# Trainium2 kernel: the end of layer 0 with five gated tiles fetched and split ahead, steps kept back for the seam behind pair 9, and the group norm at the head of the tail

## The chip, the cores and the metric

One core of a Trainium2 chip runs one launch of the kernel. The metric is the device time of a launch in microseconds (us), the median of several runs.

## The reference, cut to what matters

A trunk of two layers. Layer 0 is RWKV-7 time mixing, layer 1 differential attention; both have memory attention, a SiLU gate and an output projection. In layer 0 there are 512 prompt rows and 32 sample rows (544 columns in the kernel), 24 heads of 64 that are worked in 12 pairs, and 4 memory heads:

```
p, qm, gate = split(rmsnorm(x) @ w_in)
ps = p + mu * (p_prev - p); r, k, v, pw, pa = split(ps)
S = S * w + (S @ -kk) (kk * a)^T + v k^T; y = S @ r
y = groupnorm(y) * ln_w + ln_b + sum(r * k * r_k) * v
out = concat(y, softmax(qm @ mk^T) @ mv) * silu(gate)
x = x + out @ w_out
```

The outputs hold p's last row too (the shift state, for prompt and sample).

## The kernel before, in words

**Products.** A float32 product runs as three products of fp32r parts: hi x hi, lo x hi, hi x lo, where hi is the value cast and lo is what is left of it. ACT makes hi (CAST), VectorE (DVE) or GpSimd (POOL) subtracts and makes lo. Weights come as raw blocks of 1024 x 128, and are cast to whi and wlo as put-off work. One step of a product is one matmul of 128 x 128 by 128 x 272, and a block of weights takes 48 steps: 8 row blocks x 2 halves of the columns x 3 parts. The main stream (`stream`) of layer 0 gives such steps (tile `ps_g`, operands `hh`, `hl`, `whi`, `wlo`), and they are laid between everything else.

**The order.** Every instruction is issued in the program's order on its engine, and a helper (`tie`, L103) keeps that order; so nearly all rows carry L103 and are told apart by tiles. Layer 0 is a chain over 12 pairs. A pair has 23 entries (PLAN) of two halves; each half does a piece of the chain (`chain`: state updates, tiles `ps_c`, `avz`, `SB`), a piece of another pair's preparation (`prep`, `at`, `inv`, `mrg`, `val`: tiles `rkv`, `bk`, `bt`, `ps_v`, `ps_at`), of the group norm and the gate of the pair before (`rsq`, `fin`: tiles `yt`, `q`, `sg`, `bv`, `ps_y`), then one piece of put-off work (`some`, from the head of the list `self.later`), and then as many steps of the main stream as the planner's estimate of time gives (L1428 to L1465; MAIN is 0.126 us for a step). `until` empties the list up to a named piece. MPLAN says at which entries of pairs 10 and 11 the steps of the four memory heads (`mem_steps`, tiles `cmt`, `mhk`, `mq`, `ps_ck`, `ps_mm`, `mp`) stand.

**The seam behind pair 9** (`pr + 3 == NPAIR`, L1464). Three pieces of the preparation of pair 11 run with nothing between them, the put-off list is emptied, the memory of the preparation (`ca`) is freed and the memory heads' (`mem0a`) is opened in its place. Two transposes take the shift state (`shc`) into PSUM (`ps_sh`), ACT copies it (`sho`), and SP issues its two output transfers. The memory head's first load is `cmt`.

**The end of layer 0.** `put` stores each gated tile of 128 x 544 (`sg`) to a scratch in DRAM (`oscr`), 16 tiles in all. Behind pair 11 TAIL lists the last pieces: four pieces of `fin` (gates), `rsq` (the group norm's statistics), four times `split`, four pieces of `fin`, `out`, with 6 steps behind each. The steps come from the rest of the main stream and then from the output projection (`w_out`). `w_out` fetches gated tiles four at a time (`fetch`: `lo<-oscr`, 272 KB), and `gated` (L1159 to L1163) casts hi on ACT and makes lo in place, on DVE for an even tile and on POOL for an odd one (L1162). The projection's first two blocks are worked together: tiles 0 to 3 against block 0 (24 steps) and against block 1 (24), then tiles 4 to 7 against both, then the second eight of OUT_ORDER.

Of the kernel before, what the change touches and what calls it, by code (L numbers as in the profile page):

```python
# [17 lines left out]
P = 128  # L18
# [9 lines left out]
MH = 4  # L28
# [45 lines left out]
MPLAN = {10: [(0, 0), (1, 0), (2, 0), (3, 0), (4, 0), (5, 0), (6, 0), (6.5, 1), (7, 0), (8, 0), (9, 0), (10, 0), (10.5, 0), (12.5, 1),  # L74
# [10 lines left out]
TAIL = (("fin", 6), ("fin", 6), ("fin", 6), ("fin", 6), ("rsq", 6), ("split", 6), ("split", 6), ("split", 6), ("fin", 6),  # L85
        ("split", 6), ("fin", 6), ("fin", 6), ("out", 6))
# [19 lines left out]
class Trunk:  # L106
# [768 lines left out]

    def state_out(self, S, dst):
        nc, p = self.nc, self.rk0
        ps = self.psm.tile([P, 4, P], F32, tag="m", name="ps_so")
        self.te.transpose(ps[:, 0, :], S[:], self.ident[:])
        so = p.tile([P, 64], F32, tag="so", name="so", bufs=1)  # L880
        for h in range(2):
            hc = slice(64 * h, 64 * h + 64)
            self.ae.copy(so[hc, :], ps[hc, 0, hc])
        self.se.dma_start(dst.rearrange("h v k -> (h v) k"), so[:])
# [32 lines left out]
    def put(self, g, t):  # L917
        if not self.o1:
            self.se.dma_start(self.oscr[g // 8][:, g % 8, :], t[:])
# [239 lines left out]
    def gated(self, g, hi, lo, t):  # L1159

        self.ae.copy(hi[:], t)
        (self.nc.gpsimd if g % 2 else self.ve).tensor_tensor(lo[:], t, hi[:].bitcast(F32), ALU.subtract)  # L1162
        return hi, lo  # L1163

# [6 lines left out]
    def w_out(self, i, p, order, consume, extra=None, o=None):  # L1171
# [5 lines left out]
        def fetch():  # L1177
            if left:
                g = left.pop(0)
                came.append((g, self.fetch(p, g)))  # L1180

        def ahead(n):
            for _ in range(n):
                if came:
                    g, t = came.pop(0)
                    o[g] = self.gated(g, *t)
                    fetch()

        for _ in range(NGATED):
            fetch()  # L1190
# [65 lines left out]
    def layer0(self, mem):  # L1256
# [6 lines left out]
        with ExitStack() as ctx:  # L1263
# [69 lines left out]
            mems = [{} for _ in range(MH)]  # L1333
# [94 lines left out]
            for pr in range(NPAIR):  # L1428
                mplan = MPLAN.get(pr, ())
                took = [HOP + sum(us for x in y for kind, d, us, _ in x if 0 <= pr + d < NPAIR) for y in PLAN]  # L1430
                load = [HOPV[k % 3] + sum(us for x in y for kind, d, _, us in x if 0 <= pr + d < NPAIR) for k, y in enumerate(PLAN)]
                whole = sum(took) + MEMPE * len(mplan) / 12 + MAIN * each[pr]
# [4 lines left out]
                t, left, spent = 0.0, each[pr], 0.0  # L1437
                for k, y in enumerate(PLAN):
                    go("chain", pr)
                    t += HOP  # L1440
                    spent += HOPV[k % 3]
                    for half, x in enumerate(y):
                        for kind, d, us, vus in x:
                            if 0 <= pr + d < NPAIR and kind != "full":
                                go(kind, pr + d)
                                t += us
                                spent += vus
                        for at, h in mplan:
                            if at == k + half / 2:
                                if h not in mit:  # L1450
                                    mit[h] = self.mem_steps(mems[h], 0, h, self.ma)
                                    next(mit[h])
                                next(mit[h], None)
                                t += MEMPE / 12
                        if FULL not in x:
                            spent += self.some(room * (k + (half + 1) / 2) + 0.4 - spent)
                        while left and t + MAIN / 2 < (due[k + 1] if half else (due[k] + due[k + 1]) / 2):
                            next(main)
                            t += MAIN
                            left -= 1  # L1460
# [3 lines left out]
                if pr + 3 == NPAIR:  # L1464
                    for _ in range(3):  # L1465
                        go("prep", pr + 2)
                    while self.later:
                        self.later.pop(0)[0]()
                    ca.close()
                    self.ma = self.pool("mem0a", 1, ctx=ma, side="right")  # L1470
                    ps = self.psm.tile([P, 512], F32, tag="m", name="ps_sh")
                    so = self.ma.tile([NPROJ, 2, P], F32, name="sho")
                    for q in range(2):
                        self.te.transpose(ps[:NPROJ, q * P : q * P + P], self.shc[:, q, :], self.ident[:])
                    self.ae.copy(so[:], ps[:NPROJ, :256].rearrange("p (q c) -> p q c", q=2))
                    for q, n in ((0, 3), (1, 9)):
                        self.se.dma_start(o[n][0, 0].rearrange("(j p) -> j p", p=P), so[:, q, :])
# [5 lines left out]
            ma.close()  # L1483
            self.mp = self.pool("mem1", 1, ctx=mctx, side="right")
            mh, ml = self.mem_tiles()
            rctx.close()
        self.x1 = self.pool("x1", 1).tile([P, KT, T], F32, name="x1")
        with ExitStack() as ctx:
# [35 lines left out]
            wout, ahead = self.w_out(0, p, OUT_ORDER, consume, residual)  # L1524

            def both():
                yield from main
                for _ in range(2):
                    self.early.append(self.load(*self.ahead.pop(0)))
                yield from wout  # L1530
# [285 lines left out]
    def run(self):  # L1816
# [6 lines left out]
        self.mem = {}  # L1823
# [64 lines left out]
```

## Time and profile before

| | before |
|---|---|
| median of 3 runs | 1451.4 us (1451.32 to 1452.59) |
| the profiled execution, its own time | 1452.73 us |
| its span in the profile | 1451.0 us |
| TensorE's mean granted clock | 0.986 |
| pairs 9, 10 and 11 | about 562.7 to 706 us of the span |

A page of the profile covers one execution. PE is TensorE's matmuls, PEld its weight loads, SPq the engine SP's queue, which issues the DMAs. In a row of a timeline stand the start and the length in us, the engine, the operation, out<-in, the shape and xcount; in brackets how long the engine idled before it and what ended that (`<-`). Rows of the waits name the engine, what it was to do and whom it waited for, with the total, the times and the longest. Rows of stretches give each engine's busy time. The granted clock is the share of full speed that TensorE was given.

### The profile page before, as it was taken

The numbers are of one execution on the slowest core, as the hardware profiler recorded it, in microseconds if no ns is written. First come the engines' busy times: TensorE is split into PE (matmuls) and PEld (weight loads), VectorE is DVE, ScalarE is ACT, GpSimd is POOL, SyncE is SP. The second block draws the span as 40 slices with busy tenths as digits, with TensorE's granted clock in tenths as the row PEclk, the third lists the DMA queues.
The fourth block names the chain that finished last, engine by engine and source line by source line (L and its number), as shares of the span: only waits on it lengthen the run. The fifth ranks groups of instructions, "written<-read, shape, count | busy, mean of one in ns | idle before, by whom it ended". The sixth has DMA issues, their size and how long they took to land.

```text
span 1451.0 us, 31979 instructions
## 1 busy us (share of the span) xinstructions
PE 1397.4 (96%) x11906; PEld 1318.0 (91%) x11906; DVE 919.9 (63%) x2337; ACT 835.6 (58%) x2293; POOL 388.2 (27%) x846
## 2 busy tenths in 40 slices
PE   6998899999999999899999999999999999999997
PEld 5997899999999998788899999999999999999997
DVE  6565667787777887575743566664465745657533
ACT  6664667667776777455543366653565546664322
POOL 2025676566866567500120030000000001000200
PEclk9998999999999999999999999999999999999999
DMA  6442123323223222232554473323323222332321
GB/s 217 124 135 73 27 62 92 81 73 78 63 78 96 69 73 66 77 91 84 174 157 131 132 201 103 84 75 92 113 69 95 80 84 81 89 98 67 97 88 70
DMA packets 266533, 139.20 MB, mean 96 GB/s; under 512 B 57657, under 2 KB 256578, under 8 KB 266378
## 3 DMA queue, kind: packets, MB, share of 16 engines
q1 hardware_dynamic: 266378, 137.16, 33.4%
q8 instruction: 94, 1.54, 0.5%
q14 instruction: 61, 0.50, 0.1%
HBM read 110.98 MB, written 22.78 MB: 92 GB/s over the span
## 4 chain that ended last, share of the span: by engine, by line
PE 80%; DVE 7%; ACT 6%; issue 2%; POOL 2%; DMA 2%; SPq 1%; DVEq 0%; ACTq 0%; POOLq 0%
PE ps_g L103 57%; PE ps_c L103 4%; PE ps_s L103 2%; PE ps_o L103 2%; PE ps_at L103 2%; PE ps_mm L103 1%; PE ps_v L103 1%; DVE wlo L103 1%; PE ps_mo L103 1%; SPq L103 1%; PE ps_aT L103 1%; POOL u L723 1%; PE ps_ss L103 1%; PE ps_yc L103 1%; POOL tm L721 1%
## 5 line engine op out<-in xcount | busy, mean ns | idle before, releaser
L103 PE MATMUL ps_g<-hh,wlo 128*128 128x272 f32 x1808 | 539.5, 298 | 1.4 <-DVE wlo L103 1.4
L103 PE MATMUL ps_g<-hh,whi 128*128 128x272 f32 x1808 | 538.8, 298 | 0.0
L103 PE MATMUL ps_g<-hl,whi 128*128 128x272 f32 x1808 | 533.5, 295 | 0.0
L103 DVE TENSOR_TENSOR wlo<-raw,whi 128x512 fp32r<-128x512 f32 x322 | 224.1, 709 | 199.7 <-ACT whi L103 195.7
L103 PEld LDWEIGHTS ps_g<-hh,wlo 128*128 128x128 f32 x1808 | 342.8, 190 | 5.8 <-DVE wlo L103 2.0
L103 PEld LDWEIGHTS ps_g<-hh,whi 128*128 128x128 f32 x1808 | 343.6, 190 | 4.1
L103 PEld LDWEIGHTS ps_g<-hl,whi 128*128 128x128 f32 x1808 | 343.2, 190 | 3.9 <-issue 0.6
L103 ACT CAST whi<-raw 128x512 fp32r<-128x512 f32 x322 | 195.0, 617 | 180.5 <-PE ps_g L103 103.6
L721 POOL TENSOR_TENSOR tm<-u,m 102x84 f32<-102x84 f32 (+23 forms) x372 | 158.0, 425 | 181.1 <-DMA m<-sc 152.9
L723 POOL TENSOR_TENSOR u<-u,tm 102x84 f32<-102x84 f32 (+23 forms) x372 | 159.4, 429 | 29.1
L103 PE MATMUL ps_g<-lo,whi 128*128 128x272 f32 x512 | 148.6, 290 | 2.1 <-DVE lo L103 1.9
L103 PE MATMUL ps_g<-hi,whi 128*128 128x272 f32 x512 | 149.5, 292 | 0.8 <-ACT hi L103 0.8
L103 PE MATMUL ps_g<-hi,wlo 128*128 128x272 f32 x512 | 148.7, 290 | 0.9 <-DVE wlo L103 0.9
L1162 POOL TENSOR_TENSOR lo<-og,hi 128x544 fp32r<-128x544 f32 x8 | 13.7, 1713 | 485.8 <-DVE og L103 350.6
L103 PEld LDWEIGHTS ps_g<-lo,whi 128*128 128x128 f32 x512 | 97.2, 190 | 2.9 <-DVE lo L103 2.4
L103 PEld LDWEIGHTS ps_g<-hi,whi 128*128 128x128 f32 x512 | 97.2, 190 | 1.0 <-ACT hi L103 1.0
L103 PEld LDWEIGHTS ps_g<-hi,wlo 128*128 128x128 f32 x512 | 97.1, 190 | 1.1 <-DVE wlo L103 1.1
L103 DVE SCALAR_TENSOR_TENSOR SB<-ps_c,dl,sd 64x64 f32<-64x64 f32 x168 | 47.4, 282 | 47.4 <-PE ps_c L103 42.1
L103 ACT COPY sv<-ps_c 64x64 f32<-64x64 f32 x192 | 39.3, 205 | 39.0 <-PE ps_c L103 37.2
L103 ACT ACTIVATE pt<-ps_s,snm 128x128 f32<-128x128 f32 (+3 forms) x96 | 50.7, 529 | 18.1 <-DVE snm L103 17.0
L103 ACT ACTIVATE sg<-ps_g 128x272 f32<-128x272 f32 x64 | 25.3, 395 | 59.8 <-PE ps_g L103 59.5
L103 ACT COPY raw<-ps_g 128x272 f32<-128x272 f32 x74 | 28.6, 386 | 32.5 <-PE ps_g L103 31.8
(366 smaller groups left out, 2600.6 us busy)
## 6 DMA issues: line engine op xcount, KB each, us to landing
raw<-in_rw_in_dram SPq DMA_DIRECT2D x114, 256.0 KB
raw<-in_df_in_dram SPq DMA_DIRECT2D x112, 256.0 KB
raw<-in_w_out_dram SPq DMA_DIRECT2D x64, 256.0 KB
m<-sc SPq DMA_DIRECT2D x36, 128.0 KB
oscr<-sg SPq DMA_DIRECT2D x16, 272.0 KB
lo<-oscr SPq DMA_DIRECT2D x16, 272.0 KB
raw<-in_w_mem_k_dram SPq DMA_DIRECT2D x16, 256.0 KB
raw<-in_w_mem_v_dram SPq DMA_DIRECT2D x16, 256.0 KB
```

The lines of the kernel that those rows point to most:

```text
L103: return lambda *a, **k: self.trunk.tie(self, issue(*a, **k))
L721: nc.gpsimd.tensor_tensor(tm[:, :n, :wd], u3[:, :n, kx : kx + 1].to_broadcast(sh), m3[:, kx : kx + 1, kx + 1 :].to_broadcast(sh), ALU.mult)
L723: nc.gpsimd.tensor_tensor(u3[:, :n, kx + 1 :], u3[:, :n, kx + 1 :], tm[:, :n, :wd], ALU.add)
L1162: (self.nc.gpsimd if g % 2 else self.ve).tensor_tensor(lo[:], t, hi[:].bitcast(F32), ALU.subtract)
```

## The change

- The two transposes of `shc` (37 x 128 each) become one of 74 x 128, with one copy and the two transfers, as `shift_out`, and move from the seam to entry 13 of pair 10 (SHIFTED).
- Of pair 9's 144 main steps 24 (KEPT) aren't planned in it. Eight of them run behind each of the three pieces of `prep` in the seam.
- MPLAN of pair 10: memory head 0's steps from the second on (the one with `ps_ck`) stand an entry later, up to its last.
- In pair 10 five gated tiles (0 to 4) are fetched singly, in entries 1, 3, 5, 7 and 9, into a memory of their own (`wo0e`). Their hi (ACT) and lo (DVE) are put-off work: one in entry 18 of pair 10, four in entries 1, 5, 9 and 13 of pair 11. The projection gets them as made.
- `gated` makes layer 0's lo on DVE always; POOL takes odd ones only in layer 1.
- TAIL: all four `split` go, and 54 steps stand behind the first `fin` after `rsq`. `fetch` only fetches tiles that are stored already.
- `rctx` (layer 0's state) is closed ahead of the opening of `mem1`.

```diff
+SHIFTED, KEPT = 13, 24
+EARLY = 5
+SPLIT = {10: (18,), 11: (1, 5, 9, 13)}
-MPLAN = {10: [(0, 0), (1, 0), (2, 0), (3, 0), (4, 0), (5, 0), (6, 0), (6.5, 1), (7, 0), (8, 0), (9, 0), (10, 0), (10.5, 0), (12.5, 1),
+MPLAN = {10: [(0, 0), (2, 0), (3, 0), (4, 0), (5, 0), (6, 0), (6.5, 1), (7, 0), (8, 0), (9, 0), (10, 0), (11, 0), (11.5, 0), (12.5, 1),
-TAIL = (("fin", 6), ("fin", 6), ("fin", 6), ("fin", 6), ("rsq", 6), ("split", 6), ("split", 6), ("split", 6), ("fin", 6),
-        ("split", 6), ("fin", 6), ("fin", 6), ("out", 6))
+TAIL = (("fin", 6), ("fin", 6), ("fin", 6), ("fin", 6), ("rsq", 6), ("fin", 54), ("fin", 6), ("fin", 6), ("out", 6))
...
+    def shift_out(self):
+        ps = self.psm.tile([P, 512], F32, tag="m", name="ps_sh")
+        so = self.ma.tile([2 * NPROJ, P], F32, name="sho")
+        self.te.transpose(ps[: 2 * NPROJ, :P], self.shc[:].rearrange("p q j -> p (q j)"), self.ident[:])
+        self.ae.copy(so[:], ps[: 2 * NPROJ, :P])
+        for q, n in ((0, 3), (1, 9)):
+            self.se.dma_start(self.o[n][0, 0].rearrange("(j p) -> j p", p=P), so[q * NPROJ : q * NPROJ + NPROJ, :])
...
     def put(self, g, t):
+        self.out.add(g)
...
         self.ae.copy(hi[:], t)
-        (self.nc.gpsimd if g % 2 else self.ve).tensor_tensor(lo[:], t, hi[:].bitcast(F32), ALU.subtract)
+        (self.nc.gpsimd if g % 2 and self.o1 else self.ve).tensor_tensor(lo[:], t, hi[:].bitcast(F32), ALU.subtract)
         return hi, lo
+    def put_split(self, tiles):
+        hi, lo, t = tiles
+        self.put_off(lambda: self.ae.copy(hi[:], t))
+        self.last_split = self.put_off(lambda: self.ve.tensor_tensor(lo[:], t, hi[:].bitcast(F32), ALU.subtract), LATER)
...
-        def fetch():
-            if left:
+        def fetch(n=1):
+            while left and len(came) < n and (self.o1 or left[0] in self.out):
                 g = left.pop(0)
                 came.append((g, self.fetch(p, g)))
...
+                kept = KEPT if pr + 3 == NPAIR else 0
-                whole = sum(took) + MEMPE * len(mplan) / 12 + MAIN * each[pr]
+                whole = sum(took) + MEMPE * len(mplan) / 12 + MAIN * (each[pr] - kept)
-                t, left, spent = 0.0, each[pr], 0.0
+                t, left, spent = 0.0, each[pr] - kept, 0.0
...
+                        if half and pr == NPAIR - 2 and k == SHIFTED:
+                            self.shift_out()
+                        if half and pr == NPAIR - 2 and k % 2 and len(came) < EARLY:
+                            came.append(self.fetch(early, OUT_ORDER[len(came)]))
+                        if half and k in SPLIT.get(pr, ()):
+                            self.put_split(came[len(made)])
+                            made[OUT_ORDER[len(made)]] = came[len(made)][:2]
...
                     for _ in range(3):
                         go("prep", pr + 2)
+                        fill(KEPT // 3)
...
+                    early = self.pool("wo0e", 1, ctx=mctx, side="right")
...
             ma.close()
+            rctx.close()
             self.mp = self.pool("mem1", 1, ctx=mctx, side="right")
             mh, ml = self.mem_tiles()
-            rctx.close()
...
-            wout, ahead = self.w_out(0, p, OUT_ORDER, consume, residual)
+            wout, ahead = self.w_out(0, p, OUT_ORDER, consume, residual, made)
...
+                self.until(self.last_split)
                 yield from wout
```

The order that results, at three places. First PE in the seam: `ps_v<-ident,rkv` and `ps_bt` are the transposes of `prep`, `ps_g` are main steps. Before:

```order
L103 MATMUL ps_c<-sv,bt 128x128
L103 MATMUL ps_yc<-sv,at_90 64x64 x16
L103 MATMUL ps_v<-ident,rkv 128x128 x4
L103 MATMUL ps_bt<-ident,bk 128x128 x4
L103 MATMUL ps_sh<-ident,shc 37x128 x2
L103 MATMUL ps_c<-avz,at_91 128x128
```

The change, from the last of the 16 main steps behind the rkv transposes on:

```order
L105 MATMUL ps_g<-hh,whi 128x272
L105 MATMUL ps_bt<-ident,bk 128x128 x4
L105 MATMUL ps_g<-hl,whi 128x272
L105 MATMUL ps_g<-hh,wlo 128x272
L105 MATMUL ps_g<-hh,whi 128x272
L105 MATMUL ps_g<-hl,whi 128x272
L105 MATMUL ps_g<-hh,wlo 128x272
L105 MATMUL ps_g<-hh,whi 128x272
L105 MATMUL ps_g<-hl,whi 128x272
L105 MATMUL ps_g<-hh,wlo 128x272
L105 MATMUL ps_c<-avz,at_91 128x128
```

The shc transposes are gone from here, and 24 main steps stand between the rkv transposes and the chain's next product. `ps_ck` stood 5 main steps and the chain's pieces behind that product, and now stands 18 main steps behind it.

Second, SP's transfers in the seam (`raw` are weights, `cmt`, `mhk`, `mhv`, `cmv` the first memory head's loads, `lo_9362` and `lo_9411` the first two gated tiles). Before:

```order
L103 DMA oscr_340<-sg_83 128x544
L103 DMA out_dram<-sho 37x128 x2
L103 DMA cmt<-in_cache_mem_k_dram 128x2x128
L103 DMA mhk<-mkv_354 128x256
L103 DMA mhv<-mkv_878 128x256
L103 DMA cmv<-in_cache_mem_v_dram 128x2x128
```

The change:

```order
L105 DMA oscr_340<-sg_83 128x544
L105 DMA cmt<-in_cache_mem_k_dram 128x2x128
L105 DMA mhk<-mkv_354 128x256
L105 DMA mhv<-mkv_878 128x256
L105 DMA cmv<-in_cache_mem_v_dram 128x2x128
L105 DMA raw<-in_rw_in_dram 128x4x128 x2
L105 DMA lo_9362<-oscr_339 128x544
L105 DMA lo_9411<-oscr_339 128x544
```

cmt stands right behind the store of a gated tile; sho's two rows are in pair 10 now.

Third, DVE at the start of the output projection (`nt` and `q` are the group norm's reciprocal root, `yt` the normed values, `bv` the gated ones). Before:

```order
L103 SCALAR_TENSOR_TENSOR q_101<-nt_10638,q_101 128x20
L103 TENSOR_TENSOR lo_10589<-lo_10589,hi_10588 128x544
L103 SCALAR_TENSOR_TENSOR sg_83<-sg_83,ps_g 128x272
L103 TENSOR_TENSOR wlo<-raw,whi 128x512 x2
L103 TENSOR_TENSOR lo_10595<-lo_10595,hi_10594 128x544
L103 TENSOR_TENSOR lo_10656<-lo_10656,hi_10655 128x544
L103 TENSOR_TENSOR yt_102<-yt_102,q_101 128x640
L103 TENSOR_TENSOR lo_10688<-lo_10688,hi_10687 128x544
L103 SCALAR_TENSOR_TENSOR bv_103<-ps_y,PA,bv_103 128x512
```

The change:

```order
L105 SCALAR_TENSOR_TENSOR q_101<-nt_10665,q_101 128x20
L105 TENSOR_TENSOR yt_102<-yt_102,q_101 128x640
L105 SCALAR_TENSOR_TENSOR sg_83<-sg_83,ps_g 128x272
L105 TENSOR_TENSOR wlo<-raw,whi 128x512 x2
L105 TENSOR_TENSOR lo_10616<-lo_10616,hi_10615 128x544
L105 TENSOR_TENSOR lo_10619<-lo_10619,hi_10618 128x544
L105 TENSOR_TENSOR lo_10622<-lo_10622,hi_10621 128x544
L105 TENSOR_TENSOR lo_10625<-lo_10625,hi_10624 128x544
L105 SCALAR_TENSOR_TENSOR bv_103<-ps_y,PA,bv_103 128x512
```

yt comes first, and the four lo between wlo and bv are those of tiles 5 to 8; those of tiles 0 to 4 stand in pairs 10 and 11.

More of the change, by code (lines that the diff above doesn't have):

```diff
@@ L1183, in ahead @@
             for _ in range(n):
+                fetch()
                 if came:
@@ L1186, in ahead @@
                     o[g] = self.gated(g, *t)
-                    fetch()
-        for _ in range(NGATED):
-            fetch()
+                    fetch(depth)
+        depth = 4 if self.o1 else NGATED
+        fetch(depth)
         half = [[g for g in order if g // 8 == q] for q in range(2)]
@@ L1331, in add_mems @@
                     add(None, src, h * P, make)
-            mems = [{} for _ in range(MH)]
+            mems, came, made = [{} for _ in range(MH)], [], {}
             rw_gate = lambda pr, j: add_gate(pr, sts[j], RW_PROJ + 512 + j * P, j % 2)
@@ L1469, in layer0 @@
                     ca.close()
+                    early = self.pool("wo0e", 1, ctx=mctx, side="right")
                     self.ma = self.pool("mem0a", 1, ctx=ma, side="right")
[L1471 to L1477, printed above, removed]
             go("out", NPAIR - 1)
@@ L1822, in run @@
         self.psc = self.pool("psc", 2, space=PS)
-        self.mem = {}
+        self.mem, self.out = {}, set()
         self.ordered, self.later, self.open = False, [], []
```

## The prediction

> **What bounds the kernel now.** I read the page first, then the busy time by stretch around the edited code, then PE's waits there, then the rows one by one.
>
> ```profile
> PE 1397.4 (96%) x11906; PEld 1318.0 (91%) x11906; DVE 919.9 (63%) x2337; ACT 835.6 (58%) x2293; POOL 388.2 (27%) x846
> PE 80%; DVE 7%; ACT 6%; issue 2%; POOL 2%; DMA 2%; SPq 1%; DVEq 0%; ACTq 0%; POOLq 0%
> ```
>
> PE is busy for 96% of the span and 80% of the ending chain. The kernel has about 54 us in which PE stands still (1451.0 - 1397.4), and a change of the order can only win where PE waits or runs slowly. So the question is how much of that lies where the edit acts. The stretches (from the start of pair 9 to the first full blocks of the out-projection; columns: window, length, then busy time of PE, PEld, DVE, ACT and POOL, granted clock, DMA share, GB/s):
>
> ```profile
> 562.70:604.00 41.30, 37.51 (x378) 34.34 (x377) 31.48 (x78) 24.36 (x72) 26.62 (x66) 1.00 0.22 55
> 604.00:610.80 6.80, 3.46 (x45) 2.70 (x43) 1.07 (x4) 4.03 (x11) 5.55 (x17) 1.00 0.27 81
> 610.80:615.40 4.60, 4.60 (x23) 4.22 (x23) 0.58 (x2) 0.89 (x2) 3.58 (x14) 0.63 0.46 129
> 615.40:660.00 44.60, 43.24 (x394) 39.34 (x392) 30.10 (x78) 25.87 (x85) 0.92 (x3) 1.00 0.30 80
> 660.00:706.00 46.00, 44.12 (x364) 40.89 (x365) 29.98 (x80) 26.01 (x85) 0.00 (x0) 1.00 0.27 79
> 714.50:724.40 9.90, 7.00 (x32) 6.04 (x31) 8.53 (x14) 4.90 (x9) 4.80 (x3) 0.66 1.06 350
> 724.40:740.00 15.60, 15.60 (x127) 15.60 (x126) 9.57 (x12) 8.55 (x14) 7.39 (x5) 1.00 0.69 213
> ```
>
> Two short stretches stand out: the seam behind pair 9 (604 to 615.4) and the start of the out-projection (714.5 to 724.4). In both PE first idles and then runs with 0.63 and 0.66 of its clock; everywhere else the clock is 1.00. What PE waits for in them (total, times, longest):
>
> ```profile
> PE ps_ck L103 <- DMA cmt<-in_cache_mem_k_dram: 2.2, 1, 2.2
> PE ps_sh L103 <- ACT sv L103: 1.2, 1, 1.2
> PE ps_g L103 <- DVE lo L103: 1.9, 2, 1.2
> PE ps_g L103 <- ACT hi L103: 0.8, 1, 0.8
> ```
>
> **The seam.** The rows of PE, and below them those of ACT and of SP:
>
> ```profile
> 603.85 0.60 PE L103 MATMUL ps_bt<-ident,bk 128*128 128x128 f32 x4
> 605.60 0.41 PE L103 MATMUL ps_sh<-ident,shc 128*37 128x128 f32 x2 [1.15 <-ACT sv L103]
> 605.85 0.39 PE L103 MATMUL ps_c<-avz,at 128*128 128x128 f32 x2
> 607.84 0.29 PE L103 MATMUL ps_g<-hh,wlo 128*128 128x272 f32 x1
> 607.96 0.29 PE L103 MATMUL ps_g<-hh,whi 128*128 128x272 f32 x1
> 608.08 0.38 PE L103 MATMUL ps_c<-sv,bt 128*128 128x128 f32 x2
> 610.66 0.41 PE L103 MATMUL ps_ck<-ident,cmt 128*128 128x128 f32 x2 [2.19 <-DMA cmt<-in_cache_mem_k_dram]
> 612.05 0.43 PE L103 MATMUL ps_g<-hh,whi 128*128 128x272 f32 x1
> 612.27 0.43 PE L103 MATMUL ps_g<-hl,whi 128*128 128x272 f32 x1
> ```
> ```profile
> 604.05 1.50 ACT L103 COPY sv<-ps_v 64x256 f32<-64x256 f32 x4 [1.02 <-PE ps_v L103]
> ```
> ```profile
> 606.50 0.63 SPq L103 DMA_DIRECT2D out_dram<-sho  x2
> 607.23 0.41 SPq L103 DMA_DIRECT2D cmt<-in_cache_mem_k_dram  x1
> ```
>
> A step of the main product (ps_g) takes 0.12 us (607.84 to 607.96) at full clock and 0.22 at the lower one (612.05 to 612.27). Three things cost time here.
> - PE has four transposes of bk behind four of rkv and then nothing that doesn't need ACT's four copies of 1.50 us. It idles 1.15 us. The change lays 8 main steps (8 x 0.125 = 1.0 us) on either side of the bk transposes and 8 more earlier, 3.0 us in all: this wait goes. Taken: 1.15. The two shc transposes leave too (605.60 to 605.85: 0.25); one comes back in pair 10, so 0.12 is won.
> - PE waits 2.19 us for cmt, which SP issues only behind the two rows of sho; these wait for shc's transposes and their copy. From issue to use are 610.66 - 607.23 = 3.4 us. In the new order nothing of sho is ahead of cmt, and cmt's memory is free when the bk transposes have read. Between those and ps_ck now stand 8 main steps (1.0), the old rows from 605.85 to 608.3 (2.45), and 14 main steps (1.75): 5.2 us, against 3.4 needed. The wait goes and 1.8 us of slack remain. Taken: 2.19.
> - 610.80:615.40 has a granted clock of 0.63. If PE doesn't idle ahead of it, it runs at 1.00, as in all stretches ahead of which it didn't: 4.6 x (1 - 0.63) = 1.7.
>
> Sum of the seam: 1.15 + 0.12 + 2.19 + 1.7 = 5.2, between 3.5 (clock term stays) and 5.5 (from start to start instead of by idle times: 605.60 - 603.85 less four steps of 0.11 is 1.3, not 1.15, and 610.66 - 608.08 less two of 0.12 is 2.3, not 2.19).
>
> **What pair 9 pays.** 24 steps leave it, 3.0 us of PE's work. Where PE is the bound, the pair gets 3.0 us shorter and nothing is lost; where a chain on DVE bounds it, the hole stays open. PE's waits in pair 9, and the busy times of its first part:
>
> ```profile
> PE ps_w L103 <- DVE t1b L103: 1.2, 2, 1.0
> PE ps_c L103 <- DVE avz L103: 1.1, 1, 1.1
> PE ps_g L103 <- DVE wlo L103: 0.7, 1, 0.7
> PE ps_at L103 <- DVE bk L103: 0.6, 1, 0.6
> ```
> ```profile
> 565.00:578.00 13.00, 11.19 (x95) 10.39 (x94) 12.42 (x28) 8.90 (x27) 11.10 (x25) 1.00 0.16 43
> ```
>
> DVE fills 12.42 of these 13.0 us, so a step taken out here only lengthens a wait. 13.0 of 41.3 us hold about a third of the steps: 1.0 us. Steps ahead of the t1b and wlo waits add a little. Taken: 1.3 lost, between 0 (PE bounds all of it) and 3.0 (nothing of it).
>
> **The start of the out-projection.** Rows of PE, then DVE, ACT, POOL and SP:
>
> ```profile
> 715.53 0.39 PE L103 MATMUL ps_g<-hi,whi 128*128 128x272 f32 x1 [0.80 <-ACT hi L103]
> 716.62 0.40 PE L103 MATMUL ps_g<-lo,whi 128*128 128x272 f32 x1 [0.70 <-DVE lo L103]
> 720.78 0.59 PE L103 MATMUL ps_g<-lo,whi 128*128 128x272 f32 x1 [1.21 <-DVE lo L103]
> 723.44 1.16 PE L103 MATMUL ps_y<-ident,yt 128*128 128x128 f32 x5
> 724.35 0.37 PE L103 MATMUL ps_g<-hi,whi 128*128 128x272 f32 x1
> ```
> ```profile
> 715.85 0.72 DVE L103 TENSOR_TENSOR lo<-lo,hi 128x544 fp32r<-128x544 f32 x1
> 716.86 2.08 DVE L103 TENSOR_TENSOR wlo<-raw,whi 128x512 fp32r<-128x512 f32 x2
> 718.86 3.64 DVE L103 TENSOR_TENSOR lo<-lo,hi 128x544 fp32r<-128x544 f32 x2
> ```
> ```profile
> 714.84 0.64 ACT L103 CAST hi<-lo 128x544 fp32r<-128x544 f32 x1 [1.88 <-DMA lo<-oscr]
> ```
> ```profile
> 718.52 3.40 POOL L1162 TENSOR_TENSOR lo<-lo,hi 128x544 fp32r<-128x544 f32 x2 [0.73 <-ACT hi L103]
> ```
>
> From 715.53 to 724.35 are 8.8 us, in which PE does 24 steps (3.0 us at full clock) and five transposes of yt (0.91 us to the next row at the lower clock, so 0.45): 3.5 us of work. With the 0.8 us idle ahead of the first step, 8.8 - 3.5 + 0.8 = 6.1 us aren't work but waits and the lower clock.
>
> In the new order the first 48 steps use tiles 0 to 3, cast in pairs 10 and 11: neither hi nor lo is waited for in their 6.0 us. Meanwhile DVE does yt (0.81), wlo x2 and lo of tiles 5 to 8. DVE's lo is 0.72 where POOL is quiet (715.85), and two took 3.64 us while POOL did two of its own (718.52): with POOL's casts gone, wlo x2 (1.4) and four lo (2.9) end some 5 us behind yt, when PE still has steps of tiles 0 to 3. The second block's wlo is the close one: it comes about when its first use does. I leave 0.5 us of waits: 6.1 - 0.5 = 5.6 won, between 2.5 (waits for wlo or tile 5 take the place of the old ones, with half the clock loss) and 6.1.
>
> Seven POOL casts of 1.4 us and more that now run on DVE for 0.7 lie in 724.40:740.00, where DVE is busy for 9.57 of 15.6 us: nothing, with an end of 1.5 lost if a tile comes late.
>
> **What pairs 10 and 11 pay.** They get five hi (5 x 0.64 on ACT) and five lo (5 x 0.72 on DVE), 6.8 us in all, five fetches on SP's queue and one transpose with its copy, in 90.6 us where ACT has 51.9 and DVE 60.1 us of work (rows 615.40 and 706.00 above). DVE is idle for a third of that time. A cast that stands ahead of a chain's avz delays it by 0.7 at most, and four of five do stand there. Against that, all 30 wlo of this region, of the same length, cost PE one wait of 0.7. Between 0.2 (as wlo) and 3.0 (four of 0.72) I take 0.9, nearer to the wlo row. What is queued behind: on SP the weight loads, which are two blocks ahead. The mem step that comes an entry later, and rctx's earlier close: 0 within 0.3, since PE has main steps for it.
>
> **Sum.** 5.2 - 1.3 + 5.6 - 0.9 = 8.6 us. The profiled run took 1452.73 us (span 1451.0 and 1.7 around it), so 1444.1 by its own time; the median of the runs shown is 1.3 lower, 1451.4, and on that scale the forecast is **1442.8**.
>
> **Rivals.**
> - *The pairs are chains, not PE.* Pair 9 gives nothing back (3.0) and the casts cost 3.0: 5.2 + 5.6 - 6.0 = 4.8 won, 1446.6. For it: DVE's 12.42 of 13.0; against: PE 37.51 of 41.3 in the pair as a whole. 0.18.
> - *The clock doesn't follow the waits.* The lower clock would come again for another reason: 1.7 and in the tail 17 steps x 0.1 + 0.45 = 2.1 stay, 4.8 won, 1446.6 too. Against it: 0.63 and 0.66 stand right behind the longest waits, and waits of 1.1 in pair 9 leave 1.00. 0.05. The Trainium skill, "TensorE: Matmul & The Clock Gate", Part 1, lets the clock fall to half only after at least one idle window of some 3.4 us. By that rule a wait of 2.19 us alone wouldn't do it; the trace differs, since its longest wait here is 2.19 and the lower clock follows.
> - *The stall only moves*: cmt is still late behind SP's loads, or tile 5 and the second wlo are late in the tail. One of the two gains goes for the most part (4 to 5.6): 3 to 4.6 won, 1446.8 to 1448.4. 0.09.
> - *Slower.* The put-off work is a list that is done from its head. A tile's hi and lo stand there ahead of the next block's whi and wlo, and where the list is emptied at a block's start PE waits for all of them: 0.64 + 0.72 = 1.36, and a lower clock behind it for one window as in the seam (1.7): 3.1 for each of five splits. The gains without the casts' 0.9 are 9.5, so it decides from the fourth split on that falls so; with all five 15.3 - 9.5 = 5.8 lost, 1457. Against it: PE waits for wlo only once, 0.7. 0.10.
>
> **How the numbers follow.** Forecast 0.58, with its own range 1439.5 to 1445.5 (below: pair 9 and the casts at their low ends 2.0, seam and tail at their high ends 0.8, and a few tenths of rounding; above: half the way to the high ends of pair 9, the casts and the late tiles, 0.9 + 1.0 + 0.8). A measurement of this kernel can tell 0.2%, 2.9 us, from no change, so the bound is 1448.5. Faster: 0.58 + 0.18 + 0.05 + 0.06 = 0.87; the worse end of the third rival is within it, 0.03; slower 0.10. The range reaches from 1439.5 to the third rival's end, 1448.3.
>
> **What would show it.** Seam right: no wait of PE for cmt or sv between pair 9 and pair 10, the clock 1.00 in the 5 us behind it, cmt landed over 1 us ahead of ps_ck. Pair 9: its 41.3 us become some 39.6. Tail: no wait for hi or lo in the first 48 steps, clock 1.00, lo at 0.72 on DVE. Casts: pairs 10 and 11 longer by less than 1.5 us beside the steps they hold. Wrong: a lower clock in either place without an idle of a microsecond ahead, or wlo named as a releaser in pairs 10 and 11 more than once.

## The result and the profile after

| | before | after |
|---|---|---|
| median, runs side by side (5 and 5) | 1451.4 us (1449.39 to 1454.17) | 1445.92 us (1445.19 to 1447.59) |
| ratio, 95% interval | | 0.9955, 0.9941 to 0.9969 |
| the profiled execution's own time | 1452.73 us | 1446.66 us |
| its span | 1451.0 us | 1444.5 us |
| mean granted clock | 0.986 | 0.989 |

5.5 us were won where 8.6 were forecast: the right side and inside the range (1439.5 to 1448.3), but 0.4 us above the forecast's own range, which ends at 1445.5, and two thirds of the size. By the number alone the first rival (1446.6) is nearer; its mechanism is taken up at the end. The page's lines on PE and on the chain that ended last:

```profile
PE 1393.3 (96%) x11905; PEld 1315.6 (91%) x11905; DVE 920.0 (64%) x2345; ACT 836.4 (58%) x2293; POOL 378.6 (26%) x838
PE 76%; DVE 7%; ACT 6%; POOL 5%; issue 3%; SPq 2%; DMA 2%; DVEq 0%; POOLq 0%; ACTq 0%
```

PE stands still for 51.2 us of the span (1444.5 - 1393.3) instead of 53.6, and is busy for 4.1 us less with one matmul fewer: the smaller part of what was won is idle time, the larger is busy time, with nearly the same matmuls. The stretches of the profile after, with the columns of before:

```profile
562.70:601.40 38.70, 33.74 (x314) 30.92 (x312) 30.18 (x74) 22.95 (x70) 24.75 (x61) 0.96 0.24 59
601.40:610.60 9.20, 9.20 (x117) 8.94 (x117) 2.61 (x7) 5.49 (x14) 7.55 (x22) 1.00 0.29 84
610.60:653.50 42.90, 41.25 (x361) 38.14 (x359) 29.97 (x76) 26.62 (x87) 6.89 (x20) 1.00 0.44 125
653.50:703.30 49.80, 47.22 (x379) 42.55 (x378) 32.34 (x82) 28.01 (x90) 0.00 (x0) 1.00 0.24 73
713.80:724.00 10.20, 10.20 (x84) 10.18 (x83) 8.53 (x20) 5.55 (x10) 0.00 (x0) 1.00 0.99 309
```

Both places that idled and ran at 0.63 and 0.66 are now filled: PE is busy for 9.20 of 9.20 us in the seam and for 10.20 of 10.20 at the start of the projection, at clock 1.00. But pair 9, at 1.00 before, now has 0.96. PE's waits between 562 and 730 us:

```profile
PE ps_c L105 <- ACT yt L105: 1.9, 4, 0.6
PE ps_c L105 <- DVE avz L105: 1.4, 1, 1.4
PE ps_w L105 <- DVE t1b L105: 1.3, 2, 1.1
PE ps_c L105 <- DVE SB L105: 1.2, 2, 0.7
PE ps_at L105 <- DVE bk L105: 0.9, 1, 0.9
PE ps_g L105 <- DVE wlo L105: 0.9, 1, 0.9
```

cmt, sv, hi and lo are gone as releasers. New are SB, a longer avz and bk in pair 9, and a wlo: the one of before was in pair 9, this one is behind pair 11.

In the seam and in the tail the rows are as the forecast had them. PE and SP in the seam, then DVE and PE in the tail:

```profile
602.49 0.66 PE L105 MATMUL ps_v<-ident,rkv 128*128 128x128 f32 x4
605.00 0.60 PE L105 MATMUL ps_bt<-ident,bk 128*128 128x128 f32 x4
610.62 0.38 PE L105 MATMUL ps_ck<-ident,cmt 128*128 128x128 f32 x2
```
```profile
605.62 0.37 SPq L105 DMA_DIRECT2D cmt<-in_cache_mem_k_dram  x1
```
```profile
715.24 0.82 DVE L105 TENSOR_TENSOR yt<-yt,q 128x640 f32<-128x640 f32 x1
716.33 1.29 DVE L105 TENSOR_TENSOR wlo<-raw,whi 128x512 fp32r<-128x512 f32 x2
717.54 2.62 DVE L105 TENSOR_TENSOR lo<-lo,hi 128x544 fp32r<-128x544 f32 x4
```
```profile
719.93 0.71 PE L105 MATMUL ps_y<-ident,yt 128*128 128x128 f32 x5
```

cmt is issued right behind the bk transposes and has 5.0 us until ps_ck. Four lo take 2.62 us where two took 3.64, and yt is done 4 us ahead of the transposes that need it.

Where the time went is seen best between fixed rows of PE. The stages below run from the first `ps_yc` of a pair to the next, to the first `ps_ck`, to the projection's first step, and to the first `ps_r` (the next layer's norm):

| stage, us | before | after |
|---|---|---|
| start to end of pair 8 (same order of instructions) | 560.0 | 559.8 |
| pair 9 (24 steps fewer after) | 42.3 | 41.7 |
| seam, to ps_ck (24 steps more, ps_ck later) | 8.4 | 9.2 |
| rest of pair 10 | 45.9 | 42.9 |
| pair 11 | 48.6 | 49.8 |
| to the projection's first step | 10.4 | 10.6 |
| to the next norm | 115.0 | 109.6 |
| to the start of the last matmul (same work) | 612.4 | 612.9 |

From the end of pair 8 to the norm that is 6.8 us: 3.2 us less idle time of PE and 3.6 us less busy time. Most of the busy time is the clock: before there are three stretches of 3.41 us at half clock (one behind the seam, two in a row at the start of the projection), after there is one, in pair 9, and a stretch of 3.41 us at half clock does 1.7 us less of work. The first and the last stage hold the same work in every kernel of this study; over 13 profiles the first took 557.1 to 560.6 us and the last 611.9 to 613.0. Most stages between them repeat to 0.1 us, so they tell more than a whole run does.

### The profile page after: what moved, and what is told of

It reads as the page before. It is cut to its first block, busy times and chain, and to the rows that moved or that the text cites. A ratio compares the mean times of both kernels' runs of the same rounds, so it can differ in the third digit from the quotient of the medians.

```text
span 1444.5 us, 31982 instructions
## 1 busy us (share of the span) xinstructions
PE 1393.3 (96%) x11905; PEld 1315.6 (91%) x11905; DVE 920.0 (64%) x2345; ACT 836.4 (58%) x2293; POOL 378.6 (26%) x838
## 4 chain that ended last, share of the span: by engine, by line
PE 76%; DVE 7%; ACT 6%; POOL 5%; issue 3%; SPq 2%; DMA 2%; DVEq 0%; POOLq 0%; ACTq 0%
PE ps_g L105 54%; PE ps_c L105 4%; POOL u L725 3%; POOL tm L723 3%; PE ps_o L105 2%; PE ps_s L105 2%; SPq L105 2%; PE ps_at L105 2%; PE ps_mo L105 1%; PE ps_v L105 1%; PE ps_aT L105 1%; PE ps_mm L105 1%; DVE wlo L105 1%; PE ps_ss L105 1%; PE ps_yc L105 1%
## 5 line engine op out<-in xcount | busy, mean ns | idle before, releaser
L723 POOL TENSOR_TENSOR tm<-u,m 102x84 f32<-102x84 f32 (+23 forms) x372 | 154.2, 415 | 183.9 <-DMA m<-sc 155.8
L725 POOL TENSOR_TENSOR u<-u,tm 102x84 f32<-102x84 f32 (+23 forms) x372 | 166.7, 448 | 29.1
L1590 POOL TENSOR_TENSOR hl<-hn,hh 128x544 fp32r<-128x544 f32 x8 | 12.0, 1506 | 210.0 <-ACT hh L105 209.9
```

The source lines that it names most:

```text
L723: nc.gpsimd.tensor_tensor(tm[:, :n, :wd], u3[:, :n, kx : kx + 1].to_broadcast(sh), m3[:, kx : kx + 1, kx + 1 :].to_broadcast(sh), ALU.mult)
L725: nc.gpsimd.tensor_tensor(u3[:, :n, kx + 1 :], u3[:, :n, kx + 1 :], tm[:, :n, :wd], ALU.add)
L1590: nc.gpsimd.tensor_tensor(self.hl[:, k, :], h[:], self.hh[:, k, :].bitcast(F32), ALU.subtract)
```

## The experiments

All on the changed kernel, medians of 5 or 6 runs, seam_only of 12; the kernel before had medians of 1451.0 to 1451.6 beside them.

| run | median us | ratio to before, 95% | pair 9 | seam | pair 10 | pair 11 | to first step | to norm |
|---|---|---|---|---|---|---|---|---|
| kept0 | 1443.74 | 0.9948 (0.9936 to 0.9960) | 42.3 | 7.7 | 42.6 | 49.8 | 10.6 | 109.6 |
| from10 | 1445.02 | 0.9957 (0.9943 to 0.9971) | 42.5 | 9.0 | 42.4 | 49.8 | 10.6 | 109.6 |
| split_early | 1441.38 | 0.9932 (0.9921 to 0.9944) | 40.6 | 9.2 | 43.3 | 48.6 | 9.4 | 109.6 |
| seam_only | 1449.12 | 0.9981 (0.9972 to 0.9991) | 40.5 | 9.2 | 42.3 | 48.6 | 10.5 | 115.3 |
| direct | 1446.45 | 0.9962 (0.9949 to 0.9975) | 40.5 | 9.2 | 43.6 | 51.6 | 9.4 | 109.6 |
| split_kept0 | 1442.75 | 0.9940 (0.9926 to 0.9953) | 42.4 | 7.7 | 42.8 | 48.7 | 9.4 | 109.6 |
| split_pool | 1443.49 | 0.9946 (0.9934 to 0.9959) | 40.6 | 9.2 | 43.5 | 48.7 | 9.4 | 110.6 |
| tail_only | 1447.14 | 0.9965 (0.9953 to 0.9978) | 42.4 | 7.9 | 46.1 | 49.8 | 10.6 | 109.6 |
| budget | 1443.65 | 0.9948 (0.9935 to 0.9961) | 41.4 | 9.2 | 42.9 | 49.8 | 9.4 | 109.6 |
| low_priority | 1445.10 | 0.9961 (0.9949 to 0.9974) | 41.5 | 9.2 | 43.5 | 50.4 | 10.6 | 109.6 |
| after_again | 1444.69 | 0.9962 (0.9948 to 0.9975) | 40.5 | 9.2 | 43.0 | 49.8 | 10.6 | 109.6 |

### The two halves

**seam_only**

```diff
-EARLY = 5
-SPLIT = {10: (18,), 11: (1, 5, 9, 13)}
+EARLY = 0
+SPLIT = {}
...
-TAIL = (("fin", 6), ("fin", 6), ("fin", 6), ("fin", 6), ("rsq", 6), ("fin", 54), ("fin", 6), ("fin", 6), ("out", 6))
+TAIL = (("fin", 6), ("fin", 6), ("fin", 6), ("fin", 6), ("rsq", 6), ("split", 6), ("split", 6), ("split", 6), ("fin", 6),
+        ("split", 6), ("fin", 6), ("fin", 6), ("out", 6))
...
-        (self.nc.gpsimd if g % 2 and self.o1 else self.ve).tensor_tensor(lo[:], t, hi[:].bitcast(F32), ALU.subtract)
+        (self.nc.gpsimd if g % 2 else self.ve).tensor_tensor(lo[:], t, hi[:].bitcast(F32), ALU.subtract)
...
-                self.until(self.last_split)
```

> The seam's half of the change alone: kept steps, shift state in pair 10, memory head a step later; tail, casts and POOL's lo as before the change. If the two halves add up by the anchors of the two profiles (seam with pair 10: 5.2 won; pair 9: 2.4 lost): 2.8 won over the kernel before, about 1448.6 us, with the half clock still in 594 to 598 and again at 717 to 724. Rival (the seam's gain is returned later, where the tail's old waits are on a chain that doesn't start earlier): within 1 us of before, 1450.5 to 1451.5.

**tail_only**

```diff
-SHIFTED, KEPT = 13, 24
+SHIFTED, KEPT = 99, 0
-MPLAN = {10: [(0, 0), (2, 0), (3, 0), (4, 0), (5, 0), (6, 0), (6.5, 1), (7, 0), (8, 0), (9, 0), (10, 0), (11, 0), (11.5, 0), (12.5, 1),
+MPLAN = {10: [(0, 0), (1, 0), (2, 0), (3, 0), (4, 0), (5, 0), (6, 0), (6.5, 1), (7, 0), (8, 0), (9, 0), (10, 0), (10.5, 0), (12.5, 1),
...
                     self.ma = self.pool("mem0a", 1, ctx=ma, side="right")
+                    self.shift_out()
```

> The tail's half of the change alone: five tiles ahead, splits in pairs 10 and 11, lo on DVE, norm first; the seam as before the change (shift state's transpose there, ps_ck early, no kept steps). By the anchors: 5.3 won from the projection's first step on, 1.2 lost in pair 11 and 0.2 on the way to the first step: 3.9 won over the kernel before, 1447.1 us; the seam again waits 2.2 us for cmt and runs at half the clock for a window. Rival (the casts lag the list less when pair 10 starts with a wait): pair 11 at 48.6, 1446 us.

The halves win 0.19% and 0.35%, the change 0.45%: they add up within the intervals. tail_only came out as expected, at 1447.1. seam_only won 1.9 where 2.4 to 2.8 were expected, though by its stages it is 3.9 shorter than before up to the norm: its profiled run is the lowest of its runs, and the half clock expected in pair 9 didn't come in it (1.00); in the projection it did (711 to 718 us at 0.52). In tail_only the seam's old waits and the clock behind them are back (PE's waits from 598 to 620 us, and the stretch behind them):

```profile
PE ps_ck L105 <- DMA cmt<-in_cache_mem_k_dram: 1.8, 1, 1.8
PE ps_sh L105 <- ACT sv L105: 1.2, 1, 1.2
```
```profile
609.00:614.00 5.00, 5.00 (x27) 4.83 (x26) 1.02 (x3) 0.89 (x2) 3.98 (x14) 0.66 0.77 238
```

### Pair 9 and the kept steps

**kept0**

```diff
-SHIFTED, KEPT = 13, 24
+SHIFTED, KEPT = 13, 0
```

> The change without the 24 kept steps (they stay in pair 9, none in the seam). Theory 1 (the steps were cover for pair 9's chains, and without them its waits pile up and one window of 594 to 598 us runs at half the clock): pair 9 (from the last ps_yc of pair 8 to that of pair 9) takes 42.3 us as before the change instead of 41.7, at clock 1.00, and holds 3.0 us more work; the seam idles about 1.2 us for ACT's sv at full clock and cmt is still in time. Net 0.6 - 3.0 + 1.2 = -1.2: about 1444.7 us. Rival (the kept steps are what keeps the seam at full clock): the wait for sv lets the clock fall to half again and cmt comes late, +1.7 to +3: 1446.5 to 1448 us.

**from10**

```diff
-                kept = KEPT if pr + 3 == NPAIR else 0
+                kept = KEPT if pr + 2 == NPAIR else 0
```

> The 24 kept steps are taken from pair 10's plan instead of pair 9's; the seam stays as in the change. Theory 1 (pair 9 could not spare them): pair 9 takes 42.3 us at clock 1.00, the seam has no wait, and pair 10, whose waits were 2 to 3 us in 42, loses 0.5 to 1.5 of the 3.0: 1443.5 to 1445 us. Rival (any pair here is bounded by its chain and loses the same 2.4): 1446 us, the wait only moves to pair 10.

**after_again** (no edit)

> The change itself once more, beside the two others on the same chip: 1445.9 us within 0.8. Its first profile had a window of half clock in pair 9 (594 to 598 us) which four other profiles with the same order in pair 9 didn't have; if it depends on where the waits fall in the clock's windows, pair 9 takes 40.5 us here with the clock at 1.00, and if it belongs to the change, 41.7 again.

Pair 9 as a whole in the profile after, in after_again and in kept0, and the stretch in after where the clock falls:

```profile
559.75:601.41 41.66, 36.70 (x378) 33.62 (x378) 31.57 (x79) 25.41 (x76) 27.16 (x68) 0.96 0.26 67
594.00:598.00 4.00, 4.00 (x23) 4.00 (x22) 2.68 (x8) 2.21 (x7) 3.36 (x9) 0.57 0.00 0
```
```profile
557.45:597.96 40.51, 35.55 (x378) 32.12 (x378) 31.37 (x79) 25.35 (x76) 25.90 (x64) 1.00 0.26 68
```
```profile
558.51:600.84 42.33, 38.44 (x402) 35.10 (x401) 31.85 (x80) 25.96 (x77) 27.66 (x68) 1.00 0.26 65
```

The same 378 matmuls take 41.66 us in one execution and 40.51 in another; the difference is one window of half clock behind the t1b waits. Eight profiles have this order in pair 9: three show 0.96 and 41.4 to 41.7 us, five show 1.00 and 40.5 to 40.6. So theory 1 (the steps were cover for pair 9's chains) was half right: taking 24 steps out gives back 1.8 of their 3.0 us when the clock holds, as forecast, and 0.6 to 0.9 when it doesn't. It doesn't belong to the change in every execution.

The traces' records of the clock give a likely reason. Ahead of 1400 us each stretch of half clock in the 13 profiles is 3.41 us long or a whole multiple of it, and starts a whole number of 3.41 us from every other one of its execution (to 0.01 us): a grid that doesn't follow the program. Take the stretch from the start of the t1b wait to the end of the `ps_w` products behind it, 2.3 us. In the three profiles with the lower clock it lies within one step of that grid, but for at most 0.08 us; in the five others an edge cuts off 0.20 us or more. And a wait isn't needed. In budget and low_priority one such window came in pair 8 too, behind a step in which PE was busy for 3.35 of 3.41 us, but with small products (budget):

```profile
547.19 1.28 PE L105 MATMUL ps_ss<-hsel,sq 128*128 128x2 f32 x10
549.35 0.99 PE L105 MATMUL ps_w<-t1b,at 32*32 32x32 f32 x32
```
```profile
546.96:550.37 3.41, 3.35 (x53) 1.00 0.41 111
550.37:553.78 3.41, 3.41 (x16) 0.50 0.21 62
```

(Columns here: PE, clock, DMA share, GB/s.) These products lie within one step of the grid, but for at most 0.11 us, in these two profiles, and in none of the 11 others, where the clock stayed. This fits all profiles, but it was found in them afterwards; no run tested it.

kept0 shows the other side. Without the kept steps the seam idles:

```profile
604.17 0.33 PE L105 MATMUL ps_v<-sv,at 64*64 64x64 f32 x2 [0.93 <-ACT sv L105]
604.78 1.03 PE L105 MATMUL ps_v<-sv,at 64*64 64x64 f32 x26 [0.28 <-ACT bt L105]
```
```profile
600.00:612.00 12.00, 10.78 (x124) 10.10 (x125) 4.18 (x10) 8.38 (x24) 9.88 (x28) 1.00 0.52 162
```

These 1.2 us leave the clock at 1.00, and cmt is in time without the kept steps. The seam is 1.5 us shorter with 3.0 us less work, so the steps covered 1.5 us there; pair 9 pays 1.2 or 2.3 for it. That is nothing, or a loss: kept0's 1443.7 and 1445.9 and 1444.7 of the change can't be told apart by the intervals of their ratios, and the rival that the kept steps carry the seam's gain falls. from10 is no better: pair 9 is whole, but pair 10 gives back only 0.4 to 0.6 of the 3.0 (42.4 for 42.9 to 43.0). That is the rival's loss of 2.4, not the 0.5 to 1.5 expected. PE now waits there 1.4 us for one yt:

```profile
PE ps_c L105 <- ACT yt L105: 1.7, 2, 1.4
```

**split_kept0**

```diff
-SHIFTED, KEPT = 13, 24
-SPLIT = {10: (18,), 11: (1, 5, 9, 13)}
+SHIFTED, KEPT = 13, 0
+SPLIT = {10: (10, 13, 16, 19, 22)}
```

> All splits in pair 10 and no kept steps. If the kept steps only move cost from the seam to pair 9 (they were worth 1.5 us in the seam up to ps_ck and cost 1.3 in pair 9 where the clock stays at 1.00): the same as the splits in pair 10 with kept steps, 1441.4 us within 0.7; pair 9 42.3 us, seam 7.7 us. Rival (their seam cover is worth the whole 3.0): 1443 us. Rival on the other side (pair 9 loses its clock in many executions, so that the profile's 40.5 us flatter it): 1440 us.

1442.75 beside 1441.38 with kept steps, with intervals that overlap: by the stages 0.3 in favour of the kept steps (40.6 + 9.2 against 42.4 + 7.7) where the clock holds in pair 9, and 0.4 against them in pair 10 (43.3 and 42.8). By the stages it is the expected tie; the median is 1.4 above the 1441.4 expected, outside its 0.7 and nearer to the rival's 1443.

### The casts

**split_early**

```diff
-SPLIT = {10: (18,), 11: (1, 5, 9, 13)}
+SPLIT = {10: (10, 13, 16, 19, 22)}
```

> All five hi and lo are put off in pair 10 (entries 10, 13, 16, 19, 22) instead of one there and four in pair 11. Theory 2 (the splits in pair 11 hold up the list of put-off work, so that the last block's whi and wlo come 3.4 us later than before and PE waits 0.9 us for wlo at 705.8): that wait is gone and pair 11 is about 1 us shorter, pair 10 at most 0.3 longer: about 1445.1 us. Rival (the casts cost their time wherever they stand, or crowd pair 10's memory head): pair 10 grows by what pair 11 loses, 1446 us or more.

It won 4.5 us on the change's first median and 3.3 on the second, where 0.8 was expected. By the stages, from the end of pair 8 to the norm, it is 3.0 us shorter than the first profile of the change (260.7 against 263.7), 1.1 of them the window in pair 9. Its waits between 650 and 730 us:

```profile
PE ps_c L105 <- ACT yt L105: 0.9, 2, 0.6
PE ps_mm L105 <- DVE sg L105: 0.4, 1, 0.4
PE ps_mm L105 <- ACT so L105: 0.4, 1, 0.4
```

These are the waits of the kernel before, no more. Pair 11 is back at 48.6 and the way to the first step 9.4, a microsecond below before (whose first step waited for hi): 2.3 us together, for 0.2 to 0.4 more in pair 10. The casts of pair 11 thus cost 1.15 us in the pair and 1.14 behind it. Of the first, 0.6 are PE's waits for yt (1.3 and 0.2 us instead of 0.9); the rest wasn't traced to a row.

The second is the wait for wlo. The last whi of the main stream on ACT in the kernel before, and then after, with the rows of DVE and PE behind it:

```profile
699.19 0.62 ACT L103 CAST whi<-raw 128x512 fp32r<-128x512 f32 x1
700.07 0.62 ACT L103 CAST whi<-raw 128x512 fp32r<-128x512 f32 x1
```
```profile
697.08 0.62 ACT L105 CAST whi<-raw 128x512 fp32r<-128x512 f32 x1
703.44 0.61 ACT L105 CAST whi<-raw 128x512 fp32r<-128x512 f32 x1
```
```profile
704.46 0.69 DVE L105 TENSOR_TENSOR yt<-ps_yc,yt 128x512 f32<-128x512 f32 x1 [0.44 <-PE ps_yc L105]
705.07 1.28 DVE L105 TENSOR_TENSOR wlo<-raw,whi 128x512 fp32r<-128x512 f32 x2
```
```profile
705.80 0.39 PE L105 MATMUL ps_g<-hh,wlo 128*128 128x272 f32 x1 [0.88 <-DVE wlo L105]
```

The two whi stood 0.9 us apart and are now 6.4 apart; both wlo come behind the pair's end, when PE is already at the block. Three runs asked why.

**direct**

```diff
-        self.put_off(lambda: self.ae.copy(hi[:], t))
-        self.last_split = self.put_off(lambda: self.ve.tensor_tensor(lo[:], t, hi[:].bitcast(F32), ALU.subtract), LATER)
+        self.ae.copy(hi[:], t)
+        self.ve.tensor_tensor(lo[:], t, hi[:].bitcast(F32), ALU.subtract)
+        self.last_split = None
```

> The change, but each tile's hi and lo are issued on the spot at the same five entries (one in pair 10, four in pair 11) instead of through the list of put-off work. Theory 2 (what costs is the list: with the splits in it, the last block's second whi came at 703.4 instead of 700.1): whi and wlo come where they came before, PE doesn't wait for wlo behind pair 11, pair 11 takes 48.6 us instead of 49.8 and the way to the first step of the projection 9.4 instead of 10.6. About 2.3 better than the change, 1443.6 us. Rival (the casts themselves stand in the chain's way in pair 11): pair 11 stays at 49.8 or grows, and only the wlo wait goes: 1445 us.

The way to the first step is 9.4: outside the list the casts don't hold up wlo. But pair 11 takes 51.6, not 48.6. lo stands right behind hi here, so DVE waits for ACT's cast with the chain behind it (6.8 us in three waits for hi between 600 and 706 us), and PE's waits (660 to 720 us) show it:

```profile
PE ps_c L105 <- DVE avz L105: 1.7, 1, 1.7
```

The rival's part is right as well: in pair 11 the casts themselves stand in the chain's way. The list, which puts hi and lo at places apart, was the better form. The median, 1446.45, is 2.9 above the 1443.6 expected and 1.5 above the rival's.

**budget**

```diff
-                room = (sum(load) + 2.3 * each[pr] / 48) / len(PLAN)
+                room = (sum(load) + 2.3 * each[pr] / 48 + LATER * len(SPLIT.get(pr, ()))) / len(PLAN)
```

> The change with one term added: the planner's allowance of put-off DVE work for a pair (room) grows by 0.75 us for each split in that pair, so that the splits no longer use up what is meant for whi and wlo. Theory 3 (the lag isn't that the splits stand ahead in the list, but that the allowance doesn't count them): the last block's whi and wlo come ahead of the last pair's yt again, PE has no wlo wait behind pair 11, and the way to the projection's first step is 9.4 us instead of 10.6; with pair 11's casts as they are (49.8 or somewhat less) 1.1 to 2.3 better than the change run beside it: about 1444 us. Rival (order in the list): nothing changes, 1445.9.

**low_priority**

```diff
+        if not self.later and self.splits:
+            self.later.append(self.splits.pop(0))
...
-        self.put_off(lambda: self.ae.copy(hi[:], t))
-        self.last_split = self.put_off(lambda: self.ve.tensor_tensor(lo[:], t, hi[:].bitcast(F32), ALU.subtract), LATER)
+        self.splits.append((lambda: self.ae.copy(hi[:], t), 0.0))
+        self.last_split = lambda: self.ve.tensor_tensor(lo[:], t, hi[:].bitcast(F32), ALU.subtract)
+        self.splits.append((self.last_split, LATER))
```

> The change with the splits in a list of their own, taken only when the list of whi and wlo is empty. Theory 3 (allowance): a split still uses up the pair's allowance, the last block's wlo still comes behind the last yt, PE waits 0.9 for it, and the way to the first step stays 10.6: 1445.5 to 1446 us. Rival, theory 2 in its first form (order in the list): the wlo wait goes, 9.4 us, 1443.6.

The allowance decides. With it raised, both wlo come ahead of the pair's end (703.8) again, as in the kernel before, PE has no wait between 700 and 710 us, and the way to the first step is 9.4 (DVE in budget):

```profile
699.22 0.69 DVE L105 TENSOR_TENSOR wlo<-raw,whi 128x512 fp32r<-128x512 f32 x1
700.97 0.67 DVE L105 TENSOR_TENSOR wlo<-raw,whi 128x512 fp32r<-128x512 f32 x1
```

With a split put into the list only when no weights are in it, but the allowance as it was, the wait stays (low_priority, 700 to 710 us):

```profile
PE ps_g L105 <- DVE wlo L105: 0.9, 1, 0.9
```

So it isn't that a split stands ahead of a wlo in the list, but that each split is charged 0.75 us to an allowance that was summed without it, and the last block's wlo finds it spent. The 1.15 us in pair 11 itself are not mended by this (49.8 in budget): there only the place of the casts helped. low_priority's pairs 10 and 11 are 0.4 to 0.6 us longer than the change's; why wasn't traced.

### POOL's share

**split_pool** (the split_early kernel, and)

```diff
-        (self.nc.gpsimd if g % 2 and self.o1 else self.ve).tensor_tensor(lo[:], t, hi[:].bitcast(F32), ALU.subtract)
+        (self.nc.gpsimd if g % 2 else self.ve).tensor_tensor(lo[:], t, hi[:].bitcast(F32), ALU.subtract)
```

> All splits in pair 10, and POOL makes the lo of odd tiles 5, 7, 9, 13, 15, 11 again as before the change. Theory (two engines that subtract at once slow each other: 3.64 us for two lo of DVE and 3.40 for two of POOL before): wlo x2 goes back to about 2.1 us, two lo to 3.6, and the tiles 5 to 8 are ready no sooner; with 48 steps of cover PE waits 0 to 0.5 us: 1441.4 to 1442 us. Rival (DVE alone was what kept the start of the projection at full clock): waits for wlo or lo of over 1 us come back and the clock falls for a window, 1443 to 1445 us.

```profile
713.90 3.46 DVE L105 TENSOR_TENSOR wlo<-raw,whi 128x512 fp32r<-128x512 f32 x2
```
```profile
713.67 1.36 POOL L1174 TENSOR_TENSOR lo<-lo,hi 128x544 fp32r<-128x544 f32 x1 [94.77 <-ACT hi L105]
715.45 1.37 POOL L1174 TENSOR_TENSOR lo<-lo,hi 128x544 fp32r<-128x544 f32 x1 [0.42 <-ACT hi L105]
```
```profile
PE ps_g L105 <- DVE wlo L105: 0.8, 1, 0.8
```

Two wlo take 3.46 us beside POOL's subtractions instead of 1.29 without them, PE waits 0.8 us for wlo, and the stage to the norm is 1.0 longer; the clock stays. The median, 1443.49, is above the 1441.4 to 1442 expected and in the rival's range, but without the rival's mechanism, a wait of over 1 us and a lower clock; by the stages to the norm the run is 1.3 us longer than split_early. Of the 6.3 us that the tail wins, DVE alone is worth about 1.0; the rest belongs to the early tiles and the norm's place together, which no run separates.

## Why the prediction was right in sign and short in size

Against the forecast's terms, by the stages:

- **Seam 5.2: measured 5.7.** In seam_only, which has no casts in pair 10, seam and rest of pair 10 take 51.5 us with 3.0 us more work, before 54.3. Both waits went, and the lower clock with them. What the forecast had as one thing are two: cmt's earlier issue and ps_ck's later place hold without the kept steps (kept0: no wait for cmt, clock 1.00), and the kept steps only cover the 1.2 us of waits for sv and bt.
- **Pair 9, 1.3 lost: 1.2 with the clock at 1.00, 2.4 in the profile after**, where a window of half clock came on top. The forecast looked for the lower clock only at the two known places, not at what a longer wait would do in pair 9.
- **Start of the projection 5.6: measured 6.3** (115.0 to 109.6, and 0.9 of the first step's wait, 10.4 to 9.4 in split_early). wlo was in time, and the 0.5 us of waits left over didn't come.
- **Pairs 10 and 11, 0.9 lost: measured 2.8.** This is the term that was furthest off: 0.5 in pair 10 (42.9 against 42.3 in seam_only), 1.15 in pair 11, 1.14 behind it. The forecast's own sign, pairs 10 and 11 longer by less than 1.5 us, is missed with 1.7. The forecast took its size from the 30 wlo that cost PE one wait (they are those from pair 9 to the projection; 16 of them stand in pairs 10 and 11, and the wait is in pair 9), and judged the casts one by one by what they would delay. It left out that they are charged to an allowance which also paces whi and wlo. The rival "slower" had the releaser right (wlo late through put-off work), at one of five places, with 0.9 us and no clock behind it, but it named the order in the list, which low_priority speaks against.

5.7 - 2.4 + 6.3 - 2.8 = 6.8, the sum of the stages; without the window in pair 9 it would be 7.9, and with the casts in pair 10 as in split_early 9.7 (its stages) and 9.6 by its median. The spans of the two profiles differ by 6.5, since the first stage is 0.3 shorter and the last 0.5 longer; the medians' 5.5 has the spread of the runs in it, and what sets that was not asked.

That the result lies in the range owes something to luck: seam and projection won 1.2 us more than forecast, pair 9 and the casts cost 3.0 more. The first rival, that the pairs are chains, put 3.0 at each of the last two and came nearer to the medians' 5.5 with its 4.8 us. Its mechanism holds in part: pair 9 loses 1.2 of 3.0 with the clock at 1.00, not all, and 1.14 of the casts' 2.8 lie behind the chain, in the wait for wlo.

The Trainium skill ("TensorE: Matmul & The Clock Gate", Part 1) lets the clock fall to half after at least one idle window of some 3.4 us. The traces differ: the lower clock came behind waits of 2.2 and 1.8 us with PE at work for the rest of the 3.41 us ahead of it, and in pair 8 behind 3.35 of 3.41 us busy, so a window that is idle throughout wasn't needed. That these windows run free, as the page says, agrees with the grid of 3.41 us and with pair 9, where the same order and the same waits of 1.1 and 0.2 us had the lower clock in three of eight profiles.

split_early is the fastest version run. Its interval (0.9921 to 0.9944) lies below that of the change's second measurement and touches that of the first (0.9941 to 0.9969).

## What to carry to other kernels

Work that is moved ahead is cheap only if the place it goes to has room and if the planner there counts it: look at what else is paced by the same allowance, not only at the engine's idle share. Steps taken from one stage to cover a wait in another pay only if the giving stage is bounded by the engine that runs them; here two neighbours gave back 1.8 and about 0.5 us of 3.0. And a stage measured between two fixed instructions tells tenths of a microsecond where the whole run's spread hides two.

## What the runs showed of the hardware

- The granted clock fell to half for one window of 3.41 us behind 1.3 us of waits close together (t1b, pair 9) in three of eight profiles, behind 1.8 and 2.2 us (cmt) in both profiles that had them, behind 0.8 and 0.7 us (hi and lo at the projection, before), and not behind 0.9 and 0.3 us (kept0, split_kept0). A window cost 0.8 to 1.1 us of pair 9.
- These windows lie on a grid of 3.41 us that is fixed within an execution. In budget and low_priority one came in pair 8 behind small products (128 x 2 and 32 x 32) with PE busy for 3.35 of 3.41 us, so the idle time in a trace doesn't alone tell where the clock falls.
- Two subtractions of 128 x 512 on DVE took 1.29 us with POOL quiet (after) and 3.46 us where POOL made two of 128 x 544 of 1.36 and 1.37 us at the same time (split_pool).
